# Two matmuls of 256 columns for one of 512, in a two-layer hybrid decoder trunk

## The chip, the cores and the metric

The kernel runs on one core of a Trainium2 chip, as one program in one launch. The metric is its time on the device in microseconds (us), the median of several runs. A profile of one execution lies beside it.

## The reference

One sequence of 256 tokens, width 2048, goes through two layers. The first mixes tokens by gated linear attention in chunks of 64, the second by softmax attention with forget gates; both also attend to 256 memory tokens. After each mixer comes a gated feed-forward part whose up-projection (2048 to 2 x 5632) passes a causal convolution of width 3. Cut to what matters:

```python
def reference(x, mem, ...):
    mem_n = rmsnorm(mem, norm_mem)
    for i in range(2):
        if i == 1:
            fk, fv, fc = fox_shared_kv(x, fox_kv_norm, fox_w_kv, fox_b_f)
        mk, mv = memory_kv(mem_n, mem_w_kv[i])
        h = rmsnorm(x, norm_mix[i])
        x = x + (gla_mixer(h, mk, mv, ...) if i == 0 else fox_mixer(h, fk, fv, fc, mk, mv, ...))
        h = rmsnorm(x, norm_ffn[i])
        u = causal_dwconv(h @ ffn_w_up[i], ffn_conv_w[i], ffn_conv_b[i])
        a, val = split_cols(u, [FFN_HIDDEN, FFN_HIDDEN])
        x = x + (silu(a) * val) @ ffn_w_down[i]
    return rmsnorm(x, norm_final)
```

All of it is in float32, some 107 million weights are read once each, and nearly all the arithmetic is in products of a weight matrix with the 256 tokens.

## The kernel before

Features lie on the partitions, tokens along the columns. The residual stream is 16 tiles `x[i]` of 128 x 256. The left operand of a product is kept as two float32r parts that add up to the float32 value: `bufA[i]` and `bufB[i]` are tiles of 128 x 2 x 256, the first 256 columns the high part, the other 256 the low part (`split` makes them: a copy that rounds on ScalarE, a subtraction on VectorE).

Weights come in panels of 256 output features, cut into units of 4 chunks of 128 rows (one transfer of 512 KB from memory, on SyncE's queue). `split_unit` makes a high part `whi` (ScalarE, L188) and a low part `wlo` (VectorE, L197) of each unit, some way ahead of its use.

`proj_fm` computes one panel: two accumulators `acc[0]`, `acc[1]` of 512 columns, one for each 128 of the panel's features and each a whole PSUM bank. For each chunk, `product` issues two matmuls into an accumulator, both with a weight part as the stationary operand:

```python
TE.matmul(a, hi[:, s], both, start=done == 0, stop=False)          # L229, 512 columns
TE.matmul(a[:, :T], lo[:, s], both[:, 0, :], start=False, stop=False)   # L230, 256 columns
```

The first multiplies the high weights with both parts of the tokens at once, so that the accumulator's first half holds the product with the high part and its second half that with the low part; the second adds the low weights times the high part to the first half. In the last chunk the 512-column matmul comes after the other one (L232). `whole(a)` then adds the two halves: ScalarE copies the second half out of PSUM (L237), VectorE adds the first to it (L239). Residual updates (`add_out`) add the halves to `x` one after the other instead (L695, L696).

`proj_tm` (keys of the values, tokens on the partitions, L256 to L258) uses three matmuls of 384 or 512 columns into one accumulator; `proj_twice` is a narrow product for the gates (L276, 16 matmuls of 512 columns each, twice in the kernel). Attention itself runs in plain float32 matmuls, which are executed as two passes each. `Norm` sums squares of chunks into a 256-column tile and reduces it over the partitions with matmuls (`mean`, L312).

A scheduler sets the final order of the instructions on each engine from the program's order, priorities and its own estimates. There are eight PSUM banks: four for accumulators (`pacc`), four for small work.

Of the kernel before, what the change touches and what calls it, by code (L numbers as in the profile page):

```python
# [19 lines left out]
P = 128  # L20
# [12 lines left out]
# Segments of these lengths are cut into four parts; part i is paired with the later ones (version i).  # L33
# [13 lines left out]
# Column offsets inside fox_w_kv.  # L47
# [72 lines left out]

# Columns of the table of per-feature parameters.
# [7 lines left out]
# Columns of the table of constants.  # L129
# [6 lines left out]
def _trunk(ctx: ExitStack, tc: tile.TileContext, xt, memt, wp, wgu, gns, cnv, par, msk, out):  # L136
# [27 lines left out]
    x = [const.tile([P, T], F32, name=f"x{i}") for i in range(KC)]  # L164
    bufA = [const.tile([P, 2, T], F32R, name=f"A{i}") for i in range(KC)]
    bufB = [const.tile([P, 2, T], F32R, name=f"B{i}") for i in range(KC)]
# [33 lines left out]
    def proj_fm(key, src, evac, before=None, apart=False):  # L200
        """256 columns of a product, features on the partitions, 128 at a time."""
        units = where[key]
        total = sum(len(u[1]) for u in units)
        acc = [pacc.tile([P, 512], F32, name="acc", tag="acc") for _ in range(2)]
# [3 lines left out]
        for n, unit in enumerate(units):  # L208
# [12 lines left out]
        for c in range(2):  # L221
            for step in steps:
                product(acc[c], c, total - 1, *step)
            evac(c, acc[c])

    def product(a, c, last, done, both, hi, lo, j):
        s = slice(j * 256 + c * P, j * 256 + (c + 1) * P)
        if done < last:
            TE.matmul(a, hi[:, s], both, start=done == 0, stop=False)  # L229
        TE.matmul(a[:, :T], lo[:, s], both[:, 0, :], start=False, stop=False)  # L230
        if done == last:
            TE.matmul(a, hi[:, s], both, start=False, stop=True)  # L232

    def whole(a):
        """The two parts of a product (of the high and of the low parts of the moving operand) in one."""
        t = sm.tile([P, T], F32, name="part1", tag="part1")
        S.activation(t, a[:, T:], AF.Copy)  # L237
        r = sm.tile([P, T], F32, name="wholes", tag="wholes")
        V.tensor_tensor(r, a[:, :T], t, ALU.add)  # L239
# [23 lines left out]
    def proj_twice(key, src, width):  # L263
        """A narrow product: rows 0.. and 32.. of the result add up to it, the rest is zero."""
# [4 lines left out]
        for unit in units:  # L269
# [4 lines left out]
            for j, kc in enumerate(unit[1]):  # L274
                s = slice(j * P, (j + 1) * P)
                TE.matmul(acc, hi[:, s], src[kc], start=done == 0, stop=done == total - 1)  # L276
                done += 1
        return acc
# [10 lines left out]

    class Norm:  # L290
        """Sum of squares over chunks of features, then the reciprocal root of their mean."""
# [5 lines left out]
        def add(self, src):  # L297
            sq = sm.tile([P, T], F32, name="sq", tag="sq", bufs=2)
            S.activation(sq, src, AF.Square)
            if self.acc is None:  # L300
                self.acc = sq
            else:
                acc = sm.tile([P, T], F32, name="ssq", tag="ssq", bufs=2)
                V.tensor_tensor(acc, self.acc, sq, ALU.add)
                self.acc = acc

        def mean(self):
            """Mean of squares plus EPS, tokens on the partitions, one column per 128 tokens."""
            ps = work("t")
            for b in range(2):  # L310
                bs = slice(b * P, (b + 1) * P)
                TE.matmul(ps[:, bs], self.acc[:, bs], ones, start=True, stop=True)  # L312
# [12 lines left out]
        def col(self):  # L325
            """The reciprocal roots, tokens on the partitions."""
# [9 lines left out]
        def row(self):  # L336
            """The reciprocal roots, tokens along the columns, the same on every partition."""
            if self.r is None:
                y = self.col()
                dg = sm.tile([P, T], F32, name="dg", tag="sq", bufs=2)  # L340
# [9 lines left out]
    def softmax_tail(p, blk, rsum, pt):  # L350
        """Scales the rows of p and puts it, transposed, at its places in pt."""
# [6 lines left out]
    def mem_attention(pool, l, q, hd, dst):  # L358
        """q (scaled, negated), one head, features on the partitions."""
# [19 lines left out]
    nrm = Norm(D, "m")  # L379
    nx = Norm(D)  # L380
    with tc.tile_pool(name="load", bufs=1) as lp:
# [10 lines left out]
        def mk_out(l, j):  # L392
            def evac(c, a):
                o = mk[l][:, 2 * j + c, :]
                if l == 0:
                    S.activation(o, a[:, T:], AF.Copy)
                    V.tensor_tensor(o, o, a[:, :T], ALU.add)
                    if c == 1 and j == 1:
                        for f in range(MEM_H):
                            V.tensor_tensor(mk[0][:, f, :], mk[0][:, f, :], nrm.row(), ALU.mult)  # L400
                else:
                    V.tensor_tensor(o, whole(a), nrm.row(), ALU.mult)
# [6 lines left out]
        def first_out(c, a):  # L409
            mk_out(0, 0)(c, a)  # L410
            if c == 1:
                nc.sync.dma_start(mask[:, :M_FOX], msk[:, :M_FOX])
                sq, acc = [lp.tile([P, 4, T], F32, name=n) for n in ("sq4", "ssq4")]
                for g in range(4):
                    nc.gpsimd.tensor_tensor(sq if g else acc, mt[g], mt[g], ALU.mult)
                    if g:
                        nc.gpsimd.tensor_tensor(acc, acc, sq, ALU.add)
                V.tensor_tensor(acc[:, :2, :], acc[:, :2, :], acc[:, 2:, :], ALU.add)
                V.tensor_tensor(acc[:, 0, :], acc[:, 0, :], acc[:, 1, :], ALU.add)
                nrm.acc = acc[:, 0, :]  # L420
# [3 lines left out]
        with tc.issue_after(loads[-1].ins):  # L424
            for i in range(KC):
                nc.sync.dma_start(x[i], xt[i])
# [3 lines left out]
        for i in range(KC):  # L430
            split(bufB, i, x[i], gain("mix0", i))
            nx.add(x[i])
# [5 lines left out]
    def gla(nx):  # L438
        h, mix = bufB, bufA
        with tc.tile_pool(name="gla", bufs=1) as gp:  # L440
# [8 lines left out]
            V.tensor_tensor(glr, whole(a), nx.row(), ALU.mult)  # L449

            def take_mq(j):
                def evac(c, a):
                    q = gp.tile([P, T], F32, name="mq", tag="tmp", bufs=5)
                    V.scalar_tensor_tensor(q, whole(a), -(HD ** -0.5), nx.row(), ALU.mult, ALU.mult)
                    mem_attention(gp, 0, q, 2 * j + c, mix)
# [6 lines left out]
            def gates(hd):  # L462
                """Cumulative sums, inside chunks of 64 tokens, of TAU times the log gates."""
# [18 lines left out]
            def core(hd, q, k, v, bc):  # L482
# [73 lines left out]
                for j in range(3):  # L556
# [4 lines left out]
                    o = gp.tile([P, T], F32, name="onorm", tag="onorm", bufs=9)  # L561
                    on[3 * hd + j] = o
                    S.activation(o, po[:, :T], AF.Copy)
                    nrm.add(o)
# [5 lines left out]
            def take_og(j):  # L570
                def evac(c, a):
                    i = 2 * j + c
                    g = gp.tile([P, T], F32, name="gate", tag="tmp", bufs=5)
                    V.tensor_tensor(g, whole(a), nx.row(), ALU.mult)
                    S.activation(g, g, AF.Silu)
                    V.tensor_tensor(g, g, on[i], ALU.mult)
                    split(mix, i, g)
# [3 lines left out]
            for hd in range(GLA_H):  # L581
# [4 lines left out]
                proj_fm(("gq", hd), h, lambda c, a: V.scalar_tensor_tensor(  # L586
                    q[:, c, :], whole(a), DK ** -0.5, nx.row(), ALU.mult, ALU.mult))
                proj_fm(("gk", hd), h, lambda c, a: V.tensor_tensor(k[:, c, :], whole(a), nx.row(), ALU.mult))
# [10 lines left out]
    def fox(nx):  # L599
        hk, hq, mix = bufB, bufA, bufB  # L600
        with (
# [6 lines left out]
            V.tensor_tensor(fls, whole(a), nx.row(), ALU.mult)  # L608
# [20 lines left out]
            for j in range(6):  # L629
                proj_fm(("fk", j), hk, lambda c, a, j=j: V.tensor_tensor(kt[:, 2 * j + c, :], whole(a), nx.row(), ALU.mult))  # L630
# [6 lines left out]
            def take_mq(j):  # L637
                def evac(c, a):
                    q = fp.tile([P, T], F32, name="mq", tag="tmp", bufs=5)
                    V.scalar_tensor_tensor(q, whole(a), -(HD ** -0.5), nx.row(), ALU.mult, ALU.mult)  # L640
                    mem_attention(fp, 1, q, 2 * j + c, mix)
# [221 lines left out]
```

## Time and profile before

| | |
|---|---|
| time, median of 3 runs | 2343.29 us (2342.83 to 2343.91) |
| profiled execution, span on the core | 2341.9 us (the page gives no other time for this execution) |
| TensorE (matmul) busy | 2311.7 us, 99% |
| weight loads busy | 2021.8 us, 86% |
| VectorE busy | 1690.0 us, 72% |
| ScalarE busy | 1246.8 us, 53% |
| read from memory | 424.81 MB, 182 GB/s over the span |

In rows of the profile, PE is the matmul engine, PEld its weight loads, DVE is VectorE, ACT ScalarE, POOL GpSimd, SP the engine that issues transfers. A row of a group names line, engine, operation, the tile written and the tiles read, shape and count (x), then the busy time in us and the mean duration of one in ns, then the time for which the engine was idle just before and who ended it. A row of a timeline begins with start and duration in us; "x4" merges four that overlap or touch. The durations of matmuls overlap, since each contains the time in which the next has begun.

### The profile page before, as it was taken

Reading aid. Unit: us, or ns where it says so; the run is one execution under the profiler, and the core shown is the slowest. Engines: PE = TensorE matmul, PEld = TensorE weight load, DVE = VectorE, ACT = ScalarE, POOL = GpSimd, SP = SyncE. Lnnn points to the kernel's source line nnn. Section 1 sums busy time; section 2 is a strip of 40 time slices with the busy share of each in tenths; the row PEclk is TensorE's granted clock in tenths of the full one; section 3 lists DMA queues with packets and bytes.
Section 4 is the critical chain, followed back from the end, with each engine's and each line's share of the span. In section 5 each row is a group of like instructions: output and inputs, shape, how many; then the busy total and the mean of one; then the engine's idle time right before and its main releaser. Section 6 shows DMA issues by size and latency. Waiting matters only on the chain.

```text
span 2341.9 us, 34699 instructions
## 1 busy us (share of the span) xinstructions
PE 2311.7 (99%) x13106; PEld 2021.8 (86%) x13106; DVE 1690.0 (72%) x2847; ACT 1246.8 (53%) x1870; POOL 18.2 (1%) x24
## 2 busy tenths in 40 slices
PE   7999999999999999999999999999999999999997
PEld 6889989888888888888888888888888888888886
DVE  8677887778775777657777557677776577756776
ACT  5555555556553555445556445555554455534554
POOL 3000000000000000000000000000000000000000
PEclk9999999999999999999999999999999999999999
DMA  7545445555555555555555554465555555555553
GB/s 253 193 150 166 152 148 176 192 185 189 187 190 186 190 187 189 188 189 189 189 189 193 192 185 157 141 198 187 188 188 188 188 188 188 188 190 189 188 188 127
DMA packets 123455, 429.17 MB, mean 183 GB/s; under 512 B 13964, under 2 KB 18456, under 8 KB 123288
## 3 DMA queue, kind: packets, MB, share of 16 engines
q1 hardware_dynamic: 123000, 426.45, 54.9%
q8 instruction: 102, 1.67, 0.3%
q14 instruction: 65, 0.53, 0.1%
q10 hardware_dynamic: 288, 0.52, 0.1%
HBM read 424.81 MB, written 2.11 MB: 182 GB/s over the span
## 4 chain that ended last, share of the span: by engine, by line
PE 98%; DVE 0%; issue 0%; ACT 0%; DVEq 0%; ACTq 0%
PE acc L229 54%; PE acc L230 29%; PE acc L232 4%; PE acc L257 3%; PE acc L256 3%; PE acc L258 2%; PE ps_s L545 1%; PE ps_t L356 0%; PE ps_s L363 0%; PE ps_o L374 0%; PE ps_s L659 0%; PE ps_o L559 0%; PE ps_o L675 0%; PE ps_t L312 0%; PE acc L276 0%; PE ps_s L514 0%
## 5 line engine op out<-in xcount | busy, mean ns | idle before, releaser
L197 DVE TENSOR_TENSOR wlo<-raw,whi 128x1024 fp32r<-128x1024 f32 (+2 forms) x801 | 973.0, 1215 | 481.3 <-ACT whi L188 466.9
L188 ACT ACTIVATE whi<-raw 128x1024 fp32r<-128x1024 f32 (+2 forms) x805 | 845.5, 1051 | 833.7 <-PE acc L229 454.6
L229 PE MATMUL acc<-B,whi 128*128 128x512 f32 x2876 | 996.5, 396 | 0.9 <-DVE x L696 0.9
L229 PE MATMUL acc<-A,whi 128*128 128x512 f32 x2576 | 891.4, 397 | 7.1 <-DVE A L288 5.6
L230 PE MATMUL acc<-B,wlo 128*128 128x256 f32 x3072 | 805.5, 281 | 1.6 <-DVE wlo L197 1.6
L230 PE MATMUL acc<-A,wlo 128*128 128x256 f32 x2752 | 715.5, 281 | 8.7 <-DVE wlo L197 8.7
L229 PEld LDWEIGHTS acc<-B,whi 128*128 128x128 f32 x2876 | 524.7, 188 | 101.8 <-ACT whi L188 1.3
L230 PEld LDWEIGHTS acc<-B,wlo 128*128 128x128 f32 x3072 | 577.9, 188 | 31.5 <-DVE wlo L197 2.7
L230 PEld LDWEIGHTS acc<-A,wlo 128*128 128x128 f32 x2752 | 519.3, 189 | 38.6 <-DVE wlo L197 9.6
L229 PEld LDWEIGHTS acc<-A,whi 128*128 128x128 f32 x2576 | 469.6, 188 | 96.2 <-ACT whi L188 7.9
L237 ACT ACTIVATE part<-acc 128x256 f32<-128x256 f32 x242 | 90.9, 376 | 160.0 <-PE acc L232 159.8
L239 DVE TENSOR_TENSOR wholes<-acc,part 128x256 f32<-128x256 f32 x242 | 102.1, 422 | 63.5 <-ACT part L237 63.4
L721 ACT ACTIVATE cv<-u,cw 128x256 f32<-128x256 f32 x176 | 103.4, 590 | 0.7 <-DVE u L717 0.7
L723 DVE SCALAR_TENSOR_TENSOR cv<-u,cw,cv 128x256 f32<-128x256 f32 x176 | 84.8, 483 | 3.0
L722 DVE SCALAR_TENSOR_TENSOR cv<-u,cw,cv 128x256 f32<-128x256 f32 x176 | 84.0, 478 | 0.0
L257 PE MATMUL acc<-wlo,B 128*128 128x384 f32 (+1 forms) x224 | 81.6, 364 | 0.0
L258 PE MATMUL acc<-whi,B 128*128 128x384 f32 (+1 forms) x224 | 80.2, 358 | 0.0
L717 DVE TENSOR_TENSOR u<-wholes,row 128x256 f32<-128x256 f32 x176 | 74.3, 423 | 4.1 <-ACT row L347 1.2
L256 PE MATMUL acc<-whi,B 128*128 128x384 f32 (+1 forms) x224 | 73.3, 360 | 0.0
L232 PE MATMUL acc<-B,whi 128*128 128x512 f32 x196 | 72.4, 395 | 0.0
L695 DVE TENSOR_TENSOR x<-x,acc 128x256 f32<-128x256 f32 x128 | 49.4, 420 | 22.7 <-PE acc L232 22.7
L232 PE MATMUL acc<-A,whi 128*128 128x512 f32 x176 | 65.2, 395 | 0.0
(184 smaller groups left out, 1246.5 us busy)
## 6 DMA issues: line engine op xcount, KB each, us to landing
raw<-wp SPq DMA_DIRECT2D x771, 512.0 KB, 3.3
raw<-wp SPq DMA_DIRECT2D x32, 384.0 KB, 3.0
x<-xt SPq DMA_DIRECT2D x16, 128.0 KB, 4.8
mt<-memt SPq DMA_DIRECT2D x3, 512.0 KB, 7.0
cb<-cdram SPq DMA_DIRECT2D x12, 128.0 KB, 3.5
out<-y SPq DMA_DIRECT2D x6, 256.0 KB, 4.1
mask<-msk SPq DMA_DIRECT2D x1, 608.0 KB, 5.3
mt<-memt SPq DMA_DIRECT2D x2, 256.0 KB, 3.9
```

Of the source, the lines that this page charges most:

```text
L188: S.activation(hi[:, s], raw[:, s], AF.Copy)
L197: V.tensor_tensor(lo[:, s], raw[:, s], hi[:, s].bitcast(F32), ALU.subtract)
L229: TE.matmul(a, hi[:, s], both, start=done == 0, stop=False)
L230: TE.matmul(a[:, :T], lo[:, s], both[:, 0, :], start=False, stop=False)
L232: TE.matmul(a, hi[:, s], both, start=False, stop=True)
L237: S.activation(t, a[:, T:], AF.Copy)
L239: V.tensor_tensor(r, a[:, :T], t, ALU.add)
L256: TE.matmul(a, src[kc][:, 0, xs], hi[:, s], start=done == 0, stop=False)
L257: TE.matmul(a, src[kc][:, 0, xs], lo[:, s], start=False, stop=False)
L258: TE.matmul(a, src[kc][:, 1, xs], hi[:, s], start=False, stop=done == total - 1)
L721: S.activation(r, u[:, 2:], AF.Identity, bias=w[3], scale=w[2])
L723: V.scalar_tensor_tensor(r, u[:, :T], w[0], r, ALU.mult, ALU.add)
```

## The change

Every 512-column matmul of `proj_fm` becomes two of 256 columns that use the same weights and add into the same 256 PSUM columns: the product with the high part, that with the low part, and that of the low weights all add up in the matmul engine's accumulator. The two accumulators of a panel are the two halves of one bank. The addition of the halves (`whole`) is gone; what takes the result reads both chunks of a panel, 512 columns, in one operation where it can. The residual tiles and the split tiles are laid out in pairs for that (`x2`, `pairA`, `pairB`), and `x` is loaded by 8 transfers of two tiles in place of 16. Norms over the residual stream sum squares 512 columns at a time, so that their reduction has two products for each 128 tokens in place of one. `proj_twice` splits its 512-column matmuls too; `proj_tm` stays. The last panel of the program (`apart`) keeps two banks and finishes one chunk before the other. Comments are removed.

```diff
     def proj_fm(key, src, evac, before=None, apart=False):
...
-        acc = [pacc.tile([P, 512], F32, name="acc", tag="acc") for _ in range(2)]
+        if apart:
+            accs = [pacc.tile([P, 512], F32, name="acc", tag="acc") for _ in range(2)]
+            half = [a[:, :T] for a in accs]
+        else:
+            acc = pacc.tile([P, 512], F32, name="acc", tag="acc")
+            half = [acc[:, :T], acc[:, T:]]
...
                     for c in range(2):
-                        product(acc[c], c, total - 1, *step)
+                        product(half[c], c, total - 1, *step, first=c == 0, final=c == 1)
...
-    def product(a, c, last, done, both, hi, lo, j):
+    def product(a, c, last, done, both, hi, lo, j, first=True, final=True):
         s = slice(j * 256 + c * P, j * 256 + (c + 1) * P)
-        if done < last:
-            TE.matmul(a, hi[:, s], both, start=done == 0, stop=False)
-        TE.matmul(a[:, :T], lo[:, s], both[:, 0, :], start=False, stop=False)
-        if done == last:
-            TE.matmul(a, hi[:, s], both, start=False, stop=True)
-
-    def whole(a):
-        t = sm.tile([P, T], F32, name="part1", tag="part1")
-        S.activation(t, a[:, T:], AF.Copy)
-        r = sm.tile([P, T], F32, name="wholes", tag="wholes")
-        V.tensor_tensor(r, a[:, :T], t, ALU.add)
-        return r
+        TE.matmul(a, hi[:, s], both[:, 0, :], start=first and done == 0, stop=False, skip_group_check=True)
+        TE.matmul(a, hi[:, s], both[:, 1, :], start=False, stop=False, skip_group_check=True)
+        TE.matmul(a, lo[:, s], both[:, 0, :], start=False, stop=final and done == last, skip_group_check=True)
...
-                TE.matmul(acc, hi[:, s], src[kc], start=done == 0, stop=done == total - 1)
+                TE.matmul(acc[:, :T], hi[:, s], src[kc][:, 0, :], start=done == 0, stop=False)
+                TE.matmul(acc[:, :T], hi[:, s], src[kc][:, 1, :], start=False, stop=done == total - 1)
...
         def mean(self):
...
-                TE.matmul(ps[:, bs], self.acc[:, bs], ones, start=True, stop=True)
+                n = self.acc.shape[1]
+                for i in range(n):
+                    TE.matmul(ps[:, bs], self.acc[:, i, bs], ones, start=i == 0, stop=i == n - 1)
...
-                V.tensor_tensor(x[i], x[i], a[:, :T], ALU.add)
-                V.tensor_tensor(x[i], x[i], a[:, T:], ALU.add)
+                if len(given) == 1:
+                    V.tensor_tensor(x2[f], x2[f], given[0], ALU.add)
+                else:
+                    c, a = given
+                    V.tensor_tensor(x[2 * f + c], x[2 * f + c], a, ALU.add)
...
-                        V.tensor_tensor(u[:, 2:], whole(a), nx.row(), ALU.mult)
+                        V.tensor_tensor(u[:, :, 2:], a, twice(nx.row()), ALU.mult)
```

More of the change, by code (lines that the diff above doesn't have):

```diff
@@ L218, in proj_fm, with twice @@
                     for c in range(2):
-                        product(acc[c], c, total - 1, *step)
+                        product(half[c], c, total - 1, *step, first=c == 0, final=c == 1)
                 steps = []
[L221 to L224, printed above, removed]
-    def product(a, c, last, done, both, hi, lo, j):
-        s = slice(j * 256 + c * P, j * 256 + (c + 1) * P)
-        if done < last:
-            TE.matmul(a, hi[:, s], both, start=done == 0, stop=False)
-        TE.matmul(a[:, :T], lo[:, s], both[:, 0, :], start=False, stop=False)
-        if done == last:
-            TE.matmul(a, hi[:, s], both, start=False, stop=True)
-    def whole(a):
-        t = sm.tile([P, T], F32, name="part1", tag="part1")
-        S.activation(t, a[:, T:], AF.Copy)
-        r = sm.tile([P, T], F32, name="wholes", tag="wholes")
-        V.tensor_tensor(r, a[:, :T], t, ALU.add)
-        return r
+        if apart:
+            for c in range(2):
+                for step in steps:
+                    product(half[c], c, total - 1, *step)
+                evac(c, half[c])
+        else:
+            evac(acc.rearrange("p (c t) -> p c t", c=2))
+    def product(a, c, last, done, both, hi, lo, j, first=True, final=True):
+        s = slice(j * 256 + c * P, j * 256 + (c + 1) * P)
+        TE.matmul(a, hi[:, s], both[:, 0, :], start=first and done == 0, stop=False, skip_group_check=True)
+        TE.matmul(a, hi[:, s], both[:, 1, :], start=False, stop=False, skip_group_check=True)
+        TE.matmul(a, lo[:, s], both[:, 0, :], start=False, stop=final and done == last, skip_group_check=True)
+    def twice(t):
+        return t.unsqueeze(1).to_broadcast([P, 2, T])
     def proj_tm(key, src, evac):
@@ L392, in mk_out, with evac @@
         def mk_out(l, j):
[L393 to L400, printed above, removed]
-                else:
-                    V.tensor_tensor(o, whole(a), nrm.row(), ALU.mult)
+            def evac(a):
+                o = mk[l][:, 2 * j : 2 * j + 2, :]
+                if l == 0 and j == 0:
+                    S.activation(o, a, AF.Copy)
+                else:
+                    V.tensor_tensor(o, a, twice(nrm.row()), ALU.mult)
+                if l == 0 and j == 1:
+                    o = mk[0][:, :2, :]
+                    V.tensor_tensor(o, o, twice(nrm.row()), ALU.mult)
             return evac
@@ L407, in mv_out, with first_out @@
             return lambda b, a: S.activation(mv[l][:, b, :], a, AF.Copy, scale=nrm.col()[:, b : b + 1])
[L409 to L420, printed above, removed]
+        def first_out(a):
+            mk_out(0, 0)(a)
+            nc.sync.dma_start(mask[:, :M_FOX], msk[:, :M_FOX])
+            sq, acc = [lp.tile([P, 4, T], F32, name=n) for n in ("sq4", "ssq4")]
+            for g in range(4):
+                nc.gpsimd.tensor_tensor(sq if g else acc, mt[g], mt[g], ALU.mult)
+                if g:
+                    nc.gpsimd.tensor_tensor(acc, acc, sq, ALU.add)
+            V.tensor_tensor(acc[:, :2, :], acc[:, :2, :], acc[:, 2:, :], ALU.add)
+            nrm.acc = acc[:, :2, :]
         proj_fm(("mk", 0, 0), bufA, first_out, before=take_mem)
@@ L424, in _trunk @@
         with tc.issue_after(loads[-1].ins):
-            for i in range(KC):
-                nc.sync.dma_start(x[i], xt[i])
+            for i in range(KC // 2):
+                nc.sync.dma_start(x2[i], xt[i])
             nc.sync.dma_start(part, par)
@@ L431, in _trunk @@
             split(bufB, i, x[i], gain("mix0", i))
-            nx.add(x[i])
+            if i % 2:
+                nx.add(x2[i // 2])
         for j in range(2):
@@ L448, in gla, with evac @@
             a = proj_twice(("glr",), h, RANK)
-            V.tensor_tensor(glr, whole(a), nx.row(), ALU.mult)
+            V.tensor_tensor(glr, a, nx.row(), ALU.mult)
             def take_mq(j):
[L452 to L455, printed above, removed]
+                def evac(a):
+                    for c in range(2):
+                        q = gp.tile([P, T], F32, name="mq", tag="tmp", bufs=5)
+                        V.scalar_tensor_tensor(q, a[:, c, :], -(HD ** -0.5), nx.row(), ALU.mult, ALU.mult)
+                        mem_attention(gp, 0, q, 2 * j + c, mix)
                 proj_fm(("mq", 0, j), h, evac)
@@ L570, in take_og, with evac @@
             def take_og(j):
[L571 to L574, printed above, removed]
+                def evac(a):
+                    g = gp.tile([P, 2, T], F32, name="gate", tag="ed", bufs=2)
+                    V.tensor_tensor(g, a, twice(nx.row()), ALU.mult)
                     S.activation(g, g, AF.Silu)
-                    V.tensor_tensor(g, g, on[i], ALU.mult)
-                    split(mix, i, g)
+                    V.tensor_tensor(g, g, on[j], ALU.mult)
+                    split2(pairA, 2 * j, g)
                 proj_fm(("og", j), h, evac)
@@ L607, in fox @@
             a = proj_twice(("fl",), hk, FOX_H)
-            V.tensor_tensor(fls, whole(a), nx.row(), ALU.mult)
+            V.tensor_tensor(fls, a, nx.row(), ALU.mult)
             kt = fp.tile([P, FOX_H, T], F32, name="fkt")
@@ L629, in fox @@
             for j in range(6):
-                proj_fm(("fk", j), hk, lambda c, a, j=j: V.tensor_tensor(kt[:, 2 * j + c, :], whole(a), nx.row(), ALU.mult))
+                proj_fm(("fk", j), hk, lambda a, j=j: V.tensor_tensor(
+                    kt[:, 2 * j : 2 * j + 2, :], a, twice(nx.row()), ALU.mult))
                 for i in range(3 * j, min(3 * j + 3, KC)):
@@ L637, in take_mq, with evac @@
             def take_mq(j):
[L638 to L641, printed above, removed]
+                def evac(a):
+                    for c in range(2):
+                        q = fp.tile([P, T], F32, name="mq", tag="tmp", bufs=5)
+                        V.scalar_tensor_tensor(q, a[:, c, :], -(HD ** -0.5), nx.row(), ALU.mult, ALU.mult)
+                        mem_attention(fp, 1, q, 2 * j + c, mix)
                 proj_fm(("mq", 1, j), hq, evac)
@@ L679, in take_q, with evac @@
             def take_q(j):
-                def evac(c, a):
-                    q = fp.tile([P, T], F32, name="fq", tag="fq", bufs=3)
-                    V.scalar_tensor_tensor(q, whole(a), -(HD ** -0.5), nx.row(), ALU.mult, ALU.mult)
-                    attend(2 * j + c, q)
+                def evac(a):
+                    q = fp.tile([P, 2, T], F32, name="fq", tag="fq", bufs=2)
+                    V.scalar_tensor_tensor(q, a, -(HD ** -0.5), twice(nx.row()), ALU.mult, ALU.mult)
+                    for c in range(2):
+                        attend(2 * j + c, q[:, c, :])
                 proj_fm(("fq", j), hq, evac)
@@ L692, in add_out, with evac @@
         for f in range(8):
-            def evac(c, a, f=f):
-                i = 2 * f + c
-                V.tensor_tensor(x[i], x[i], a[:, :T], ALU.add)
-                V.tensor_tensor(x[i], x[i], a[:, T:], ALU.add)
+            def evac(*given, f=f):
+                if len(given) == 1:
+                    V.tensor_tensor(x2[f], x2[f], given[0], ALU.add)
+                else:
+                    c, a = given
+                    V.tensor_tensor(x[2 * f + c], x[2 * f + c], a, ALU.add)
                 if then is not None:
-                    then(i)
+                    for c in range(2) if len(given) == 1 else given[:1]:
+                        then(2 * f + c)
             proj_fm((*key, f), src, evac, apart=key == ("down", 1, len(PARTS) - 1) and f == 7)
@@ L738, in then @@
                 split(dst, i, x[i], gain(name, i))
-            n.add(x[i])
+            if i % 2:
+                n.add(x2[i // 2])
         return n, then
@@ L759, in then @@
         def then(i):
-            fin.add(x[i])
+            if i % 2:
+                fin.add(x2[i // 2])
             if i == KC - 1:
```

78 lines of the change are left out of this document (43 added, 35 removed).

## The prediction

> **What bounds the kernel now.** I read the page first (busy times, chain, groups), then the waits of the matmul engine, then a table of one stage, then single stretches of the timeline.
>
> ```profile
> span 2341.9 us, 34699 instructions
> PE 2311.7 (99%) x13106; PEld 2021.8 (86%) x13106; DVE 1690.0 (72%) x2847; ACT 1246.8 (53%) x1870; POOL 18.2 (1%) x24
> PE 98%; DVE 0%; issue 0%; ACT 0%; DVEq 0%; ACTq 0%
> ...
> L229 PE MATMUL acc<-B,whi 128*128 128x512 f32 x2876 | 996.5, 396 | 0.9 <-DVE x L696 0.9
> L229 PE MATMUL acc<-A,whi 128*128 128x512 f32 x2576 | 891.4, 397 | 7.1 <-DVE A L288 5.6
> L230 PE MATMUL acc<-B,wlo 128*128 128x256 f32 x3072 | 805.5, 281 | 1.6 <-DVE wlo L197 1.6
> L230 PE MATMUL acc<-A,wlo 128*128 128x256 f32 x2752 | 715.5, 281 | 8.7 <-DVE wlo L197 8.7
> ...
> L237 ACT ACTIVATE part<-acc 128x256 f32<-128x256 f32 x242 | 90.9, 376 | 160.0 <-PE acc L232 159.8
> L239 DVE TENSOR_TENSOR wholes<-acc,part 128x256 f32<-128x256 f32 x242 | 102.1, 422 | 63.5 <-ACT part L237 63.4
> ```
>
> The matmul engine is busy 99% of the span and carries 98% of the chain that ended last. There are as many weight loads as matmuls (13106 each), so a matmul never reuses the weights of the one before it. VectorE and ScalarE have spare time. The waits of the matmul engine for others, all of them:
>
> ```profile
> PE acc L230 <- DVE wlo L197: 10.3, 3, 8.7
> PE acc L229 <- DVE A L288: 5.6, 1, 5.6
> PE ps_s L771 <- ACT xg L764: 1.7, 2, 1.3
> PE acc L229 <- ACT whi L188: 1.4, 1, 1.4
> PE acc L229 <- DVE x L696: 0.9, 1, 0.9
> ```
>
> They add up to 19.9 us (total, times, longest), and the two largest single ones, 8.7 and 5.6, wait for the splits of weights and of the memory tokens, which the change leaves alone. So the whole of what lighter evictions could give back on the path is 19.9 - 8.7 - 5.6 = 5.6 us. Everything else in this case is the pace of a stream of matmuls.
>
> The duration in a row is not that pace, because matmuls overlap: 996.5 + 891.4 + 805.5 + 715.5 us is more than the span. What counts is start to start. The groups of the matmul engine inside 600 to 700 us (feed-forward stage of the first layer), where nothing else ran on it:
>
> ```profile
> L229 PE MATMUL acc<-B,whi 128*128 128x512 f32 x210 | 71.6, 395 | 0.0
> L230 PE MATMUL acc<-B,wlo 128*128 128x256 f32 x227 | 57.4, 279 | 0.0
> L229 PE MATMUL acc<-A,whi 128*128 128x512 f32 x60 | 20.6, 394 | 0.0
> L230 PE MATMUL acc<-A,wlo 128*128 128x256 f32 x61 | 15.7, 279 | 0.0
> L232 PE MATMUL acc<-B,whi 128*128 128x512 f32 x16 | 5.9, 394 | 0.0
> L232 PE MATMUL acc<-A,whi 128*128 128x512 f32 x2 | 0.6, 400 | 0.0
> ```
>
> 210 + 60 + 16 + 2 = 288 matmuls of 512 columns and 227 + 61 = 288 of 256: 100 us / 288 = 347.2 ns for a pair. That is the price of one weight chunk today.
>
> **The change, part by part.** (1) Each pair of 512 + 256 columns becomes three matmuls of 256. The columns are the same, 768; what is added is one matmul instruction with its weight load for each of 3072 + 2752 = 5824 pairs. So the question is whether a matmul has a fixed cost beside its columns. Two places show it. First, sixteen 512-column matmuls in a row (the narrow product) and what follows them:
>
> ```profile
> 110.80 3.79 PE L276 MATMUL acc<-B,whi 128*128 128x512 f32 x16
> 114.42 0.62 PE L229 MATMUL acc<-B,whi 128*128 128x512 f32 x2
> ```
>
> From 110.80 to 114.42 is 3.62 us for 16, that is 226 ns each. Against the pair, 347 - 226 leaves 121 for a 256-column matmul: more than half of 226, which is 113. Two equations, 512 c + f = 226 and 768 c + 2 f = 347, give a fixed part f of 16 ns and c = 0.41 ns a column; with 0.6 ns of doubt in each of the two readings f is good to some 3 ns. Second, the nearest thing to the new stream: a few places where the order happens to put four or five 256-column matmuls behind each other.
>
> ```profile
> 420.58 0.75 PE L230 MATMUL acc<-A,wlo 128*128 128x256 f32 x5
> 421.17 0.40 PE L229 MATMUL acc<-A,whi 128*128 128x512 f32 x1
> ...
> 689.66 0.64 PE L230 MATMUL acc<-A,wlo 128*128 128x256 f32 x4
> 690.13 0.40 PE L229 MATMUL acc<-A,whi 128*128 128x512 f32 x1
> ```
>
> Start to next start: 0.59 / 5 = 118 ns and 0.47 / 4 = 117.5 ns. The first step of such a run comes right after a 512 and is shorter; taking the four alone, 0.64 us less the last one's own 0.28 is 0.36 us for three steps, 120 ns. A dense stream should therefore run at 118 to 121 ns a matmul; I take 120, since in the changed kernel no 512 stands ahead of them. Three cost 360 ns against 347.7 (the mean of 347.2 here and 348.2 in the window below). 5824 x 12.3 ns = +71.6 us. At 118 it would be 354 and +37 us, at 121.7 (347.7 less 226) 365 and +101 us.
>
> ```profile
> L229 PE MATMUL acc<-A,whi 128*128 128x512 f32 x268 | 91.7, 395 | 0.0
> L230 PE MATMUL acc<-A,wlo 128*128 128x256 f32 x286 | 73.5, 280 | 0.0
> L232 PE MATMUL acc<-A,whi 128*128 128x512 f32 x18 | 6.7, 394 | 0.0
> L344 PE MATMUL ps_t<-dg,mask 128*128 128x256 f32 x2 | 0.6, 378 | 0.0
> ```
>
> (1600 to 1700 us: 286 pairs beside two others of some 0.4 us, so 99.6 / 286 = 348.2.)
>
> The Trainium skill, "TensorE: Matmul & The Clock Gate", section "Back-to-back issue gap", puts the fixed part of a full-speed matmul at 2.5 ns (columns / 2.4 + 2.5); by that the split would cost about 5824 x 2.5 = 15 us, an estimate from the page. The sixteen matmuls at 226 ns instead of the page's 216 say otherwise, and the measurement decides.
>
> Adding into the same columns three times in a row, and both chunks of a pair in one bank, I price at nothing: the sixteen matmuls at 226 ns all add into one bank and the same columns.
>
> (2) The evictions. The 242 copies of L237 (90.9 us of ScalarE) and the 242 additions of L239 (102.1 us of VectorE) go, and pairs of 256-wide operations become single 512-wide ones. All this lies beside the matmuls, which hide it today; the two engines had 28% and 47% of the span free, and they get more. On the path it can give back at most the 5.6 us above. I take 1 us. In turn the second chunk's eviction no longer starts ahead of anything; both chunks end within one chunk's time in either kernel, and four banks now hold four pairs instead of two, so I see no new wait.
>
> (3) Small terms. The narrow products become 32 x 2 matmuls of 256: 32 x (240 - 226) = 0.4 us. Six of the ten norms now sum two accumulators: six more times two products, each of two passes. One such norm of today, with the row work ahead of it:
>
> ```profile
> 2328.86 0.42 DVE L696 TENSOR_TENSOR x<-x,acc 128x256 f32<-128x256 f32 x1
> 2329.37 0.42 ACT L299 ACTIVATE sq<-x 128x256 f32<-128x256 f32 x1 [0.90 <-DVE x L696]
> ...
> 2329.82 0.43 DVE L304 TENSOR_TENSOR ssq<-ssq,sq 128x256 f32<-128x256 f32 x1 [0.54 <-ACT sq L299]
> ...
> 2330.59 1.06 PE L312 MATMUL ps_t<-mask,ssq 128*128 128x128 f32 x4
> ```
>
> Four passes take at most 1.06 us, so six norms add at most 6.4 us, and at least 6 x 4 x 0.1 = 2.4 (0.1 us is what 128 columns need at twice the 0.41 ns). I take 2.6. At the very end, one addition of 0.42 us goes (L696), while the square and the sum become 512 wide, at most 0.42 + 0.43 more, so the tail moves by -0.4 to +0.4: nothing.
>
> Sum: +71.6 - 1 + 0.4 + 2.6 = +73.6 us on the profiled span of 2341.9, 2415.5. The page gives no time of its own for that execution beyond the span; the median of the runs, 2343.3, is 1.4 us above it, which I carry over: 2417 us, 3.1% slower.
>
> **The rivals.** A: *an extra matmul is nearly free.* A 256-column matmul between two of 512 advances the stream by less than 120:
>
> ```profile
> 1003.23 0.28 PE L230 MATMUL acc<-A,wlo 128*128 128x256 f32 x1
> 1003.34 0.39 PE L229 MATMUL acc<-A,whi 128*128 128x512 f32 x1
> 1003.57 0.28 PE L230 MATMUL acc<-A,wlo 128*128 128x256 f32 x1
> 1003.69 0.39 PE L229 MATMUL acc<-A,whi 128*128 128x512 f32 x1
> ```
>
> Here 3.23 to 3.34 and 3.57 to 3.69 are 110 and 120 ns, 115 in the mean, so the 512s take 230. If 116 to 117 were its true price, three cost 348 to 351: +2 to +19 us, with the small terms 2347 to 2364; the page's 2.5 ns, +15 us, falls in here as well. Against it: the runs of four and five. Chance 9%.
>
> B, the other side: *the columns stream faster in 256s.* If the shortest step after a 256 (the 110 to 113 ns above) held throughout, three cost 339, -8.7 ns a chunk: 5824 x -8.7 = -51 us, 2295. It decides from below 115 ns a matmul. For it speaks only that step; against it that the same runs go on at 120. Lighter evictions alone cannot make it faster, as 5.6 us is all they can give. Chance 6%.
>
> C: *issue or weight loading becomes the bound.* Six instructions in 360 ns is one every 60 ns, where today it is four in 347 ns, one every 87. The densest 10 us of the trace:
>
> ```profile
> 233.00:243.00 10.00, 10.00 (x63) 9.06 (x62) 8.57 (x23) 5.83 (x9) 0.00 (x0) 1.00 0.52 168
> ```
>
> 63 matmuls and 62 loads, one instruction every 80 ns; a long stretch at 60 isn't in the trace. If a load and a matmul together needed 125 ns, three cost 375: 5824 x 27.3 = +159 us, 2504; it decides from 120 ns a pair upwards. Against it: runs of four at 120. The Trainium skill (same page, Part 1) has a matmul cost about 62 ns of the sequencer where its hardware decode is off; were it so here and for loads too, 124 ns a pair and about 2487 us would follow, an estimate from the page; no row here shows it. Chance 13%.
>
> That the change does not do what it says I can put aside: the program's order for the changed kernel has 5824 x 3 matmuls of 256 columns with no 512 left in these products.
>
> **How the numbers follow.** Forecast 72%, A 9%, B 6%, C 13%. About 0.2% (5 us) is what a measurement of this kernel can tell from no change. The forecast's own range runs from 118 to 121.7 ns a matmul, 2382 to 2446. The range given, 2375 to 2475, adds the milder half of C (up to 123 ns a matmul: 369, 5824 x 21.3 = +124 us, 2469) and leaves out A, B and the worse half of C, some 20%. Faster: B, 6%. Within 0.2%: the lower end of A, 4%. Slower: the rest, 90%.
>
> **What would show it.** Right: in a 100 us window of the feed-forward stage about 277 triples (831 matmuls of 256) instead of 288; some 19,000 loads; the matmul engine still at 99%; L237 and L239 gone without the chain moving; VectorE's share well below 72% and no shorter span for it. Wrong: a triple at 350 ns or less (A, B), or at 370 and more with gaps that no semaphore ends (C), or new waits of matmuls on evictions.

## The result, and the profile after

The changed kernel takes 2407.3 us (median of 4 runs, 2406.97 to 2407.86) against 2343.45 (4 runs): 2.71% slower, ratio 1.0271 with a 95% interval of 1.0256 to 1.0285. The forecast was 2417 with 2375 to 2475.

From the page of the changed kernel:

```profile
span 2405.2 us, 45393 instructions
PE 2374.7 (99%) x18986; PEld 2346.4 (98%) x18986; DVE 1525.0 (63%) x2239; ACT 1159.8 (48%) x1576; POOL 18.0 (1%) x20
PE 98%; ACT 0%; DVE 0%; DMA 0%; issue 0%; DVEq 0%; ACTq 0%; SPq 0%
PE acc L243 29%; PE acc L241 29%; PE acc L242 29%; PE acc L264 2%; PE acc L265 2%; PE acc L263 2%; PE ps_s L560 1%; PE ps_t L372 0%; PE ps_t L328 0%; PE ps_o L390 0%; PE ps_s L379 0%; PE ps_s L677 0%; PE ps_o L574 0%; PE ps_o L693 0%; PE ps_s L529 0%
...
L241 PE MATMUL acc<-B,whi 128*128 128x256 f32 x3072 | 871.6, 284 | 0.0
L243 PE MATMUL acc<-B,wlo 128*128 128x256 f32 x3072 | 870.6, 284 | 0.7 <-DVE wlo L201 0.7
L242 PE MATMUL acc<-B,whi 128*128 128x256 f32 x3072 | 870.9, 284 | 0.0
```

The matmul engine carries 98% of the chain, as it did. It does 18986 matmuls and 18986 weight loads: a matmul with the same weights as the one before it loads them again. VectorE lost 165 us and ScalarE 87, and the span grew by 63.3.

The waits of the matmul engine for others, after:

```profile
PE acc L243 <- DVE wlo L201: 11.9, 3, 7.2
PE acc L241 <- ACT whi L192: 6.3, 1, 6.3
PE ps_s L794 <- ACT xg L787: 1.4, 1, 1.4
PE acc L264 <- DVE wlo L201: 0.6, 2, 0.4
```

That is 20.2 us in place of 19.9. Names have changed (the first matmul of the program waits 6.3 us for `whi`, before it waited 5.6 for `A`), the sum has not; the difference is pace. The same 100 us of the feed-forward stage, the kernel before first, then the changed one (matmuls and loads in brackets behind their busy time, then VectorE and ScalarE):

```profile
600.00:700.00 100.00, 100.00 (x576) 87.33 (x574) 76.57 (x121) 56.68 (x84) 0.00 (x0) 1.00 0.58 188
```

```profile
600.00:700.00 100.00, 100.00 (x836) 100.00 (x835) 67.43 (x94) 50.95 (x70) 0.00 (x0) 1.00 0.56 185
```

The view counts every matmul that reaches into the window. Of the 576 before, 573 begin in it, which makes 348.9 ns a pair from start to start; of the 836 after, 834 begin in it, 120.0 ns apart in the mean. Four of them and the loads beside them, from the timeline:

```profile
600.02 0.28 PE L241 MATMUL acc<-B,whi 128*128 128x256 f32 x1
600.14 0.28 PE L242 MATMUL acc<-B,whi 128*128 128x256 f32 x1
600.26 0.28 PE L243 MATMUL acc<-B,wlo 128*128 128x256 f32 x1
600.38 0.28 PE L241 MATMUL acc<-B,whi 128*128 128x256 f32 x1
```

```profile
600.02 0.19 PEld L242 LDWEIGHTS acc<-B,whi 128*128 128x128 f32 x1
600.14 0.19 PEld L243 LDWEIGHTS acc<-B,wlo 128*128 128x128 f32 x1
```

The load for the next matmul begins with the one before it. Each step is 120 ns, and in the whole trace 96% of the steps of these lines are exactly that. The granted clock is 1.00 in both windows.

### The profile page after: what moved, and what is told of

It is laid out like the page before. It is cut to its first block, busy times and chain, and to the rows that moved or that the text cites. A ratio compares the mean times of both kernels' runs of the same rounds, so it can differ in the third digit from the quotient of the medians.

```text
span 2405.2 us, 45393 instructions
## 1 busy us (share of the span) xinstructions
PE 2374.7 (99%) x18986; PEld 2346.4 (98%) x18986; DVE 1525.0 (63%) x2239; ACT 1159.8 (48%) x1576; POOL 18.0 (1%) x20
## 4 chain that ended last, share of the span: by engine, by line
PE 98%; ACT 0%; DVE 0%; DMA 0%; issue 0%; DVEq 0%; ACTq 0%; SPq 0%
PE acc L243 29%; PE acc L241 29%; PE acc L242 29%; PE acc L264 2%; PE acc L265 2%; PE acc L263 2%; PE ps_s L560 1%; PE ps_t L372 0%; PE ps_t L328 0%; PE ps_o L390 0%; PE ps_s L379 0%; PE ps_s L677 0%; PE ps_o L574 0%; PE ps_o L693 0%; PE ps_s L529 0%
## 5 line engine op out<-in xcount | busy, mean ns | idle before, releaser
L241 PE MATMUL acc<-B,whi 128*128 128x256 f32 x3072 | 871.6, 284 | 0.0
L243 PE MATMUL acc<-B,wlo 128*128 128x256 f32 x3072 | 870.6, 284 | 0.7 <-DVE wlo L201 0.7
L242 PE MATMUL acc<-B,whi 128*128 128x256 f32 x3072 | 870.9, 284 | 0.0
L243 PE MATMUL acc<-A,wlo 128*128 128x256 f32 x2752 | 781.3, 284 | 11.1 <-DVE wlo L201 11.1
L241 PE MATMUL acc<-A,whi 128*128 128x256 f32 x2752 | 781.8, 284 | 6.3 <-ACT whi L192 6.3
L242 PE MATMUL acc<-A,whi 128*128 128x256 f32 x2752 | 781.5, 284 | 0.0
L243 PEld LDWEIGHTS acc<-B,wlo 128*128 128x128 f32 x3072 | 589.0, 192 | 1.2 <-DVE wlo L201 0.9
L242 PEld LDWEIGHTS acc<-B,whi 128*128 128x128 f32 x3072 | 589.4, 192 | 0.3
L241 PEld LDWEIGHTS acc<-B,whi 128*128 128x128 f32 x3072 | 589.0, 192 | 0.3
L241 PEld LDWEIGHTS acc<-A,whi 128*128 128x128 f32 x2752 | 529.9, 193 | 6.5 <-ACT whi L192 6.3
L242 PEld LDWEIGHTS acc<-A,whi 128*128 128x128 f32 x2752 | 530.1, 193 | 0.2
L737 DVE TENSOR_TENSOR u<-acc,row 128x512 f32<-128x512 f32 x88 | 60.8, 691 | 55.0 <-PE acc L243 55.0
L744 DVE SCALAR_TENSOR_TENSOR cv<-u,cw,cv 128x256 f32<-128x256 f32 x176 | 77.0, 478 | 0.0
L745 DVE SCALAR_TENSOR_TENSOR cv<-u,cw,cv 128x256 f32<-128x256 f32 x176 | 76.9, 478 | 0.1
L714 DVE TENSOR_TENSOR x<-x,acc 128x512 f32<-128x512 f32 x63 | 43.3, 687 | 46.6 <-PE acc L243 46.5
```

The costliest lines, as they stand in the source:

```text
L241: TE.matmul(a, hi[:, s], both[:, 0, :], start=first and done == 0, stop=False, skip_group_check=True)
L242: TE.matmul(a, hi[:, s], both[:, 1, :], start=False, stop=False, skip_group_check=True)
L243: TE.matmul(a, lo[:, s], both[:, 0, :], start=False, stop=final and done == last, skip_group_check=True)
L737: V.tensor_tensor(u[:, :, 2:], a, twice(nx.row()), ALU.mult)
L744: V.scalar_tensor_tensor(r, u[:, c, 1 : T + 1], w[1], r, ALU.mult, ALU.add)
L745: V.scalar_tensor_tensor(r, u[:, c, :T], w[0], r, ALU.mult, ALU.add)
```

## Experiments

The theory: each matmul costs a fixed time beside its columns, so a third one for each chunk costs that once more. Matmuls of 512 columns among themselves take 226.7 ns a step (226 or 227 in the trace of before), those of 256 take 120; that makes 0.417 ns a column and 13.3 ns beside the columns. Rivals: the shared bank and the new evictions cost it; or 120 ns is a floor that a load and its matmul cannot go below.

**Split alone.** The kernel before, with its evictions and two banks:

```diff
-            TE.matmul(a, hi[:, s], both, start=done == 0, stop=False)
+        TE.matmul(a[:, :T], hi[:, s], both[:, 0, :], start=done == 0, stop=False, skip_group_check=True)
+        TE.matmul(a[:, T:], hi[:, s], both[:, 1, :], start=False, stop=False, skip_group_check=True)
...
```

> The kernel before with each 512-column matmul made as two of 256, into the two halves of the accumulator as they were: two banks, the addition of the halves and all evictions stay. Theory 1 (every matmul has a fixed cost of some 13 ns beside its columns): three at 120 ns, about +60 us, 2400 to 2410 us. Theory 3 (the time comes from adding three times into the same 256 columns of one bank, or from the new evictions): no such cost here, 2340 to 2350 us. Theory 2 (a floor of 120 ns for a load and its matmul) gives the same as theory 1 here.

2403.63 us, ratio 1.0253 (1.0239 to 1.0267), with VectorE as busy as ever:

```profile
span 2401.8 us, 46224 instructions
PE 2372.0 (99%) x18930; PEld 2342.8 (98%) x18930; DVE 1689.9 (70%) x2847; ACT 1229.5 (51%) x1870; POOL 18.0 (1%) x24
```

So the split itself makes the loss, in other banks and other columns too. What remains of the change, the shared bank, the narrow products and the paired evictions with their longer norms, is +3.7 us by the two medians; the intervals overlap, so its sign isn't settled. The shared bank is no part of it that the traces show: the mean step of these matmuls is 120.7 ns in both.

**Evictions alone.** The kernel before, without the addition of the halves (the second half is left out of the result):

```diff
     def whole(a):
-        t = sm.tile([P, T], F32, name="part1", tag="part1")
-        S.activation(t, a[:, T:], AF.Copy)
-        r = sm.tile([P, T], F32, name="wholes", tag="wholes")
-        V.tensor_tensor(r, a[:, :T], t, ALU.add)
-        return r
+        return a[:, :T]
...
-                V.tensor_tensor(x[i], x[i], a[:, T:], ALU.add)
```

> The kernel before with its 512-column matmuls, but without the addition of the two halves (the second half, the product with the low part of the tokens, is left out of the result): ScalarE and VectorE lose about 193 us of work. If lighter evictions give time back, this shows how much at most: I expect -1 us, between 0 and -5.6 us, 2338 to 2343 us. If the evictions were a hidden part of the bound, -10 us or more.

2342.39 against 2344.47 us, ratio 0.9993 (0.9984 to 1.0002), though VectorE fell by 153 us and ScalarE by 84:

```profile
span 2341.1 us, 33975 instructions
PE 2311.2 (99%) x13106; PEld 2023.0 (86%) x13106; DVE 1537.4 (66%) x2477; ACT 1162.6 (50%) x1628; POOL 18.1 (1%) x24
```

Work taken off engines that are not the bound is worth 2 us here by the medians, and no more than 4 by the interval.

**Six matmuls of 128 columns.** The changed kernel, its products inside a loop over the two halves of the tokens:

```diff
-        TE.matmul(a, hi[:, s], both[:, 0, :], start=first and done == 0, stop=False, skip_group_check=True)
+        for t in range(0, T, P):
+            h = slice(t, t + P)
+            TE.matmul(a[:, h], hi[:, s], both[:, 0, h], start=first and done == 0 and t == 0, stop=False,
+                      skip_group_check=True)
...
```

> The changed kernel with each 256-column matmul made as two of 128, six in place of three; the result is whole. Theory 1 (fixed 13.3 ns each): 53.3 + 13.3 = 66.7 ns a matmul, 400 ns for six against 360, +40 x 5824 = +233 us, about 2640 us. Theory 2 (a floor of 120 ns for a weight load and its matmul, whatever the columns): 720 ns for six, about 4500 us. A floor of 107 ns for the load alone: 640 ns, about 4040 us.

4243.74 us (ratio 1.810, 1.807 to 1.813): the theory in its plain form fell. Steps:

```profile
600.00 0.27 PE L243 MATMUL acc<-B,whi 128*128 128x128 f32 x1
600.11 0.27 PE L245 MATMUL acc<-B,whi 128*128 128x128 f32 x1
600.22 0.28 PE L246 MATMUL acc<-B,wlo 128*128 128x128 f32 x1
600.33 0.28 PE L243 MATMUL acc<-B,whi 128*128 128x128 f32 x1
```

Half the columns take 111 ns in place of 120. There is a floor, below 120 and above the 67 that columns plus 13.3 ns would need. Is it the load, or the issue of two instructions?

**Narrow loads.** The changed kernel, second and third matmul cut:

```diff
+        q = slice(s.start, s.start + 64)
-        TE.matmul(a, hi[:, s], both[:, 1, :], start=False, stop=False, skip_group_check=True)
-        TE.matmul(a, lo[:, s], both[:, 0, :], start=False, stop=final and done == last, skip_group_check=True)
+        TE.matmul(a[:64, :P], hi[:, q], both[:, 1, :P], start=False, stop=False, skip_group_check=True)
+        TE.matmul(a[:64, :P], lo[:, q], both[:, 0, :P], start=False, stop=final and done == last,
+                  skip_group_check=True)
```

> The changed kernel with the second and third matmul of each triple on 64 weight columns and 128 tokens only (half of the features and half of the tokens are left out there); the first stays at 128 weight columns and 256 tokens. It asks what makes the floor of some 112 ns that six matmuls of 128 columns showed. Theory L (the weight load is the floor, in proportion to its columns): steps of 120 ns (256 columns, then a 64-column load), about 67 ns (128 columns plus 13.3, a 64-column load takes less) and 112 ns (128 columns, then a 128-column load): 299 ns a triple, about 2050 us. Theory I (issue of a load and a matmul is the floor, 112 ns however many columns): 120, 112 and 112: 344 ns, about 2310 us. If the 13.3 ns beside the columns were itself a part of the load, the first step would be about 113 in place of 120.

1996.67 us (one run). Matmuls, then loads:

```profile
600.10 0.33 PE L242 MATMUL acc<-A,whi 128*128 128x256 f32 x1
600.26 0.22 PE L243 MATMUL acc<-A,whi 128*64 128x128 f32 x1
600.32 0.22 PE L244 MATMUL acc<-A,wlo 128*64 128x128 f32 x1
600.38 0.34 PE L242 MATMUL acc<-A,whi 128*128 128x256 f32 x1
```

```profile
600.04 0.19 PEld L242 LDWEIGHTS acc<-A,whi 128*128 128x128 f32 x1
600.14 0.14 PEld L243 LDWEIGHTS acc<-A,whi 128*64 128x64 f32 x1
600.27 0.14 PEld L244 LDWEIGHTS acc<-A,wlo 128*64 128x64 f32 x1
600.33 0.19 PEld L242 LDWEIGHTS acc<-A,whi 128*128 128x128 f32 x1
```

It is the load, by these rows. The 128-column load holds the next one off for 108 ns (600.04 to 600.14 at this reading, 108 in the trace's nanoseconds), a 64-column one for about 60 where nothing else does (600.27 to 600.33). A triple takes 289 ns (from the starts between 600 and 700 us), so a load and its matmul take 96 in the mean, less than the 111 above: the issue of instructions isn't that floor. The Trainium skill, "TensorE: Matmul & The Clock Gate", section "LDWEIGHTS (loading the stationary operand)", puts a load at columns / 1.2 ns, an estimate of 107 ns for 128 columns. The trace agrees with its 108. The split into single steps came out otherwise than expected (170, 59, 60 and not 120, 67, 112). Perhaps the row of a matmul can begin before its load has ended (the row of L242 begins at 600.38, its load at 600.33 with 0.19); that is our reading and was not tested. The sum, 289, is 10 under the 299 of theory L. A step of 59 ns for 128 columns (53 ns of columns at 0.417 each) leaves 6 ns beside them, not 13: so the 13.3 may belong to the load as well.

**Half loads.** As above, but with all tokens:

```diff
+        TE.matmul(a[:64], hi[:, q], both[:, 1, :], start=False, stop=False, skip_group_check=True)
+        TE.matmul(a[:64], lo[:, q], both[:, 0, :], start=False, stop=final and done == last, skip_group_check=True)
```

> The changed kernel with all 256 tokens in every matmul, but 64 weight columns in the second and third of each triple (half of the features are left out there). It asks whether the 13 ns that a float32r matmul of 256 or more columns takes beside its columns goes with the matmul or with the weight load. With the matmul: 120 ns each, 360 a triple, 2405 us as the changed kernel. With the load, in proportion to its columns (the 59 ns of a 128-column matmul with a 64-column load speak for that): 120 + 2 x 113.3 = 346.7 ns a triple, about 2330 us.

2339.78 us (one run; the kernel before beside it 2345.2): as fast as the kernel before, with 45% more matmuls than it.

```profile
600.06 0.28 PE L242 MATMUL acc<-B,whi 128*128 128x256 f32 x1
600.17 0.28 PE L243 MATMUL acc<-B,whi 128*64 128x256 f32 x1
600.29 0.28 PE L244 MATMUL acc<-B,wlo 128*64 128x256 f32 x1
600.41 0.28 PE L242 MATMUL acc<-B,whi 128*128 128x256 f32 x1
```

A triple takes 350 ns here, near 346.7 and far from 360. Between 700 and 1150 us it takes 346.7 exactly; one window of that stretch, of whose 868 matmuls 865 begin in it:

```profile
800.00:900.00 100.00, 100.00 (x868) 100.00 (x867) 70.49 (x100) 52.72 (x73) 0.00 (x0) 1.00 0.56 191
```

So the fixed part goes with the number of weight columns loaded: 40 ns for 3 x 128 in the changed kernel, some 29 for 256 in the kernel before (348.9 less 320) and, in three loads, 27 to 30 here: 0.10 to 0.12 ns a column in each. One rival stands: a matmul with 64 weight columns also writes 64 partitions in place of 128, and no run changes one without the other. That the cost belongs to the load and not to the narrower output is argued from the floor above, not shown.

**bfloat16.** The high and low parts in bfloat16, in the changed kernel and in the kernel before:

```diff
-F32R = mybir.dt.float32r
+F32R = mybir.dt.bfloat16
...
-                V.tensor_tensor(lo[:, s], raw[:, s], hi[:, s].bitcast(F32), ALU.subtract)
+                V.tensor_tensor(lo[:, s], raw[:, s], hi[:, s], ALU.subtract)
```

> The changed kernel with the high and low parts of weights and tokens in bfloat16 in place of float32r (fewer bits of the products are kept). If the 13.3 ns beside the columns belong to float32r: 256 columns in 106.7 + 2.5 = 109 ns, 327 ns a triple, about 2215 us. If they belong to every matmul: 360 ns, 2407 us. If a floor of 112 ns for the load holds for bfloat16 too: 336 ns, about 2265 us.

> The kernel before with the same four parts in bfloat16. If the 13.3 ns belong to float32r: 216 + 109 = 325 ns a pair, about 2195 us, so that splitting the 512-column matmul costs about 15 us there in place of 64. If they belong to every matmul: 347 ns, about 2343 us, and the split costs 64 us there too.

2210.51 and 2193.27 us (two runs each). The split costs 17 us there. Steps of the changed kernel in bfloat16, and a load:

```profile
600.03 0.27 PE L241 MATMUL acc<-B,whi 128*128 128x256 bf16 x1
600.13 0.27 PE L242 MATMUL acc<-B,whi 128*128 128x256 bf16 x1
600.24 0.27 PE L243 MATMUL acc<-B,wlo 128*128 128x256 bf16 x1
600.35 0.27 PE L241 MATMUL acc<-B,whi 128*128 128x256 bf16 x1
...
600.03 0.10 PEld L242 LDWEIGHTS <-whi 128*128 128x128 bf16 x1
```

0.32 us for three at this reading, 109.2 ns a step in the mean over the trace: 2.5 ns beside the columns. The formula of the Trainium skill that the prediction weighed ("TensorE: Matmul & The Clock Gate", section "Back-to-back issue gap", columns / 2.4 + 2.5) gives an estimate of 109.2 ns for 256 columns. The bfloat16 steps agree with it, the 120 ns of float32r do not. The float32r loads are also twice as long in their rows (0.19 against 0.10).

**Two orders of the kernel before.** The irregular steps that lift a pair from 346.7 to about 350 ns were put down to the order. Low weights first, almost strictly alternating (two of a kind, 512 or 256, follow each other in 41 places, in the kernel before in 1411):

```diff
...
+        TE.matmul(a[:, :T], lo[:, s], both[:, 0, :], start=done == 0, stop=False, skip_group_check=True)
+        TE.matmul(a, hi[:, s], both, start=False, stop=done == last, skip_group_check=True)
```

> The kernel before with the low weights' matmul of 256 columns ahead of the 512-column one in every chunk, so that the order on the matmul engine is strictly alternating (before, some 700 places have two of a kind in a row). If a matmul costs its columns and a fixed 13.3 ns, a pair is 346.7 ns everywhere against about 352 in the mean over the whole kernel with its waits: 2312 to 2330 us. If the irregular steps have nothing to do with the order, no change: 2343.

2341.95 us, ratio 0.9989 (0.9980 to 0.9997): a miss. But the mean hides two rhythms of the same order:

```profile
800.00:900.00 100.00, 100.00 (x579) 87.48 (x578) 79.76 (x127) 59.32 (x91) 0.00 (x0) 1.00 0.59 190
1050.00:1150.00 100.00, 100.00 (x568) 86.67 (x567) 77.99 (x125) 56.87 (x87) 0.00 (x0) 1.00 0.58 185
```

From start to start a pair takes 346.7 ns in the first window (steps of 230 to 233 and 112 to 118) and 353.5 in the second, where each third 512 takes 241. The stream went over after one of the 41 places, at 954 us; the same kind of place at 688 us had changed nothing. So the price of columns and 13.3 ns a matmul is reached with 512s and 256s in turn; which rhythm the stream falls into is open.

And the matmuls of a unit in two blocks:

```diff
+                for part in "hl":
+                    for step in steps:
+                        for c in range(2):
+                            product(acc[c], c, total - 1, *step, part)
...
```

> The kernel before with the matmuls of a unit of four chunks in two blocks: the eight of 512 columns first, then the eight of 256. If the 3 ns a pair that the trace of before shows above 346.7 come from the change between 512 and 256 columns, a block of sixteen takes 8 x 226.7 + 8 x 120 = 2773 ns, 346.7 a pair, and the kernel loses 15 to 25 us: 2318 to 2328 us. If they have another cause, 2343 us as before.

2339.15 us, ratio 0.9978 (0.9969 to 0.9988): 4.4 us faster, a quarter of what was expected. Blocks of eight:

```profile
601.01 1.12 PE L233 MATMUL acc<-B,wlo 128*128 128x256 f32 x8
601.96 2.00 PE L231 MATMUL acc<-B,whi 128*128 128x512 f32 x8
603.80 1.11 PE L233 MATMUL acc<-B,wlo 128*128 128x256 f32 x8
```

The 256s take 0.95 / 8 = 119 ns, but the 512s 1.84 / 8 = 230 and not 226.7: in a block they go 233, 236, 228, 233, 231 before they settle at 226 to 227. What costs those nanoseconds is open. Of the versions run here it is the fastest that keeps the precision.

## Why the prediction was right

The forecast case happened, for the reason given (a cost beside the columns for each further matmul with its load), and the forecast was 10 us too high.

- *Three at 120 ns.* Measured 120, flat. The prediction's runs of four and five 256-column matmuls had shown it; the single steps of 110 to 120 between 512s, on which rivals A and B rested, were no price of their own, since the 512 beside them took the rest.
- *A pair at 347.7 ns.* This is the mis-sized term. The prediction divided its windows by all matmuls listed, and the list holds those that only reach into a window; from start to start a pair takes 348.9 ns in the first and about 349.5 in the second. The rest of the gap lies outside the two windows, where other work stands between the products. From all matmul starts after the first 30 us, a pair of before takes 352.2 ns and a triple of after 362.0, both with what little waiting there is: 9.8 ns, or 57 us over 5824, in place of 12.3 and 71.6. The changed kernel has none of the irregular steps (230 to 241 ns for a 512) that the kernel before pays for.
- *The rest.* With the first 30 us the products make +58 of the 63.3 us between the two spans. The other 5 stand against 2.0 in the forecast. That is luck: with 2.0 the forecast would have been 13 us too high and not 10. The norms' matmuls take 2.0 to 2.2 us more and the narrow products 0.6, the first matmul comes 0.6 later, `proj_tm` takes 0.9 more (each from matmul start to next start); what is left, about 1 us, has no one place.
- *Evictions, -1 us.* -2.1 measured without the additions, with an interval that holds zero; the bound of 5.6 us, read from the waits, held.
- *Norms and narrow products, +3.0 us.* No run changes them alone; the traces give 2.6 to 2.8. The last norm has twice the passes:

```profile
2393.65 1.16 PE L328 MATMUL ps_t<-mask,ssq 128*128 128x128 f32 x8
```

  Eight passes end after 1.16 us, at 112 ns for all steps but the first, where four took 1.06 at 214 ns a step.
- *Rival A* (nearly free) is out for float32r and true for bfloat16. *Rival B* (256s faster) is out. *Rival C* (issue or loads as the bound) is out at 256 columns, but was nearer than its 13% said: the floor of a load lies at 108 to 112 ns, a tenth under the 120, and at 128 columns it decides everything. The 10 us that the prediction called the densest are not: from 227.96 to 237.96 us the view lists 68 matmuls and 67 loads, one instruction every 74 ns, which is still short of 60.
- What the prediction called a fixed part of a matmul goes with the columns of its load. For this change both give the same number, as each new matmul brings a whole load of 128 columns.

## What to carry to other kernels

In a stream that is bound by the matmul engine, read start to start, never the rows' durations or the number of rows that a window lists, and take the price of a new stream from places of the same shape in a row, not from single steps between others. Widen the moving side rather than repeat the weights: with float32r every further load of 128 weight columns cost 13 ns at 256 moving columns, and at 128 the load itself (108 to 112 ns) became the pace. Relieving engines with spare time is worth at most the waits on them that the profile lists, here some 2 us for 237 us of work.

## What the runs showed of the hardware that was not expected

- The cost beside the columns of a float32r matmul goes with the weight columns loaded (or with the partitions written, which changed with them): 128 moving columns took 59 ns in single steps with 64-column loads, 111 in a stream with 128-column loads; a triple of 256 took 360 ns with three full loads and 346.7 to 350 with one full and two half loads.
- In bfloat16 the same program runs at 109 ns for 256 columns and 2193 us in all for the kernel before: 6.4% less (ratio 0.9357, 0.9338 to 0.9375), at fewer kept bits.
- 512-column float32r matmuls take 226.7 ns among themselves but up to 241 when 256s stand between or before them, and the same order of 512s and 256s ran at 346.7 ns a pair in one stretch and at 353.5 in another; why stays open.
